# A hybrid encoder block: order of two products in the last token quad of a block pair, weight slots in that order, and a buffer of its own for the row diagonals

## The chip, the cores and the metric

The kernel runs on one core of one Trainium2 chip. The metric is device time in microseconds (us) of one execution; the median of several executions is compared. The engines of the core are TensorE (PE in the profile, with its weight loads as PEld), VectorE (DVE), ScalarE (ACT), GpSimd (POOL) and the queues that issue DMAs (SPq on SyncE, ACTq on ScalarE).

## What is computed

One layer over 2048 tokens of width 1024. All groups read one normalised input through one combined projection, each is multiplied by its gate, and an output projection, a residual and a last norm follow. Cut to what matters here:

```python
h = rmsnorm(x, norm_g[l])
proj = h @ w_in[l]
qk_raw, v, o, z_a, gates, u, z_b, qc, z_c = jnp.split(proj, _OFFS, axis=-1)
y_a = mlstm_branch(qk_raw, v, o, ig, fg, ...) * jax.nn.silu(z_a)
y_b = pool_branch(u, pool_w[l], pool_scale[l]) * jax.nn.silu(z_b)
y_c = mem_attn_branch(qc, mem, mem_norm_g[l], w_mem_kv[l]) * jax.nn.silu(z_c)   # softmax over 256 memory rows
x = x + jnp.concatenate([y_a, y_b, y_c], axis=-1) @ w_out[l]
return rmsnorm(x, final_norm_g)
```

The columns `v`, `o` and `z_a`, of 512 each, are made token by token (rows of tokens on the partitions); the change is in how their products are ordered.

## The kernel before, in words

**Tiling.** The 2048 tokens are four blocks of 512. Two blocks make a pair, and the projection of a pair is made by a scheme of Strassen's kind: seven products in place of eight for each "quad" (two blocks of tokens by two column blocks, over two halves of the width). The seven products are named by their input form (`A11`, `A12`, `S1`, `S2`, `S3`, `S4`, `A22`) and their weight form (`B11`, `B21`, `T1`, `T2`, `T3`, `B22`, `N4`). `T1` is a plain difference of two weight blocks, `T2` takes `T1` off a third. `S1`, with `T1`, is the input form that is a plain sum. Every fp32 operand is split into a high and a low part, and a product is three matmuls for each tile (`mm3`, lines 151 to 156): high by high, high by low, low by high. A product of a token quad is 48 matmuls: two banks (`bk`), in each two tiles of 128 tokens, four slices of the width and the three parts.

**A token quad** is `run_tok`, lines 390 to 448. It goes through the seven products in the order of a table (`TOK_ORDER`, line 49). A product writes two PSUM banks. `A11` and `A12` accumulate in the banks `P` and `S1` and `S4` in `V`, both under the PSUM tag `mm`, of which there are four banks. `S2` writes `U`, and `S3` and `A22` write `W`, both under the tag `pt`, of which there are two banks. ACT copies `P` away after `A11` into `s1` (line 418) and makes the first output `c11` from it after `A12` (line 421); DVE makes `u2` from `U` after `S2` (line 425) and turns `s1` into `V + u2` after `S1` (line 427); the other three outputs follow at lines 430, 436 and 442, each stored from ACT's queue (line 397). The tags `s1` and `u2` have two buffers each in SBUF; `c11` and the row diagonals `dg` take buffers of `u2` in turn.

**Order.** Per pair: a mixed stage (channel quads with convolution and pooling), then `attention_stage` (line 911) with four attention quads and one token quad, that with index `i == 2` (`z_a`, function Silu). This token quad runs while the softmax of the last head is still under way: `attend` (line 746) puts its scores, its transposes into two `pt` banks (`transposes`, line 770) and its product with the memory values (`pv`, line 785) a counted number of steps ahead (`later`, `tick`). The transposed probabilities are split by ACT (line 781) and DVE (line 782) and leave the `pt` banks by that. The order in which each engine gets its instructions is then made from this program by a planner that runs the program on a simulated clock and takes, on each engine, the earliest written instruction that it holds to be ready (`schedule_with_timeline_sim=True`); a few instructions are tied behind the one written before them on their engine (`keep_in_program_order`).

**Between the pairs.** After the first pair's quad with index 2 comes the first pair's quad with index 1, called with `turn` (line 941): it loads the second pair's raw input (`y`, line 181), multiplies it by the row norms (`scale_y`, line 183) and splits it into the new forms, each into the slots that the old form has just left. The row norms are spread over the partitions by `bcast` (line 163): DVE writes four diagonal blocks into `dg`, and one PE matmul against ones (line 168) puts them into a bank of tag `aux`. `scale_y` runs it twice, for block 2 and for block 3. Then come the second pair's quads 1 and 0. The weight forms of quad 1 are read back from DRAM (line 285) into eight slots (`wf`), of which a form takes two, as slots become free.

**Beside the second pair's quad with index 2** the output weights are loaded and split (`prep_wo`, line 966), into input slots in the order of the table `wslots` (line 963) as the forms `A12`, `S2`, `S1` and so on are done with them.

Of the kernel before, what the change touches and what calls it, by code (L numbers as in the profile page):

```python
# [15 lines left out]
ALU = mybir.AluOpType  # L16
AX = mybir.AxisListType

P = 128
# [28 lines left out]
            ("S1", "T1", "V", True), ("S3", "T3", "W", True), ("S4", "B22", "V", False), ("A22", "N4", "W", False))  # L48
TOK_ORDER = (("A11", "B11", "P", True), ("A12", "B21", "P", False), ("S2", "T2", "U", True),
             ("S1", "T1", "V", True), ("S3", "T3", "W", True), ("S4", "B22", "V", False), ("A22", "N4", "W", False))  # L50


def hybrid_block(tc, xT, xn, memT, wch, wuT, wtok, wgt, wkm, wvm, wo, pw, cols, bg, gf, out):
# [33 lines left out]
    with ExitStack() as outer:  # L87
# [72 lines left out]
            V.tensor_scalar(ms[:, :w], src, 1.0 / n, EPS, ALU.mult, ALU.add)  # L160
            G.tensor_tensor(dst, ms[:, :w], mhalf[:, :w], ALU.pow)

        def bcast(src_cols, w):
            dg = ev("dg", shape=(P, 4, P), tag="u2")
            for i in range(w):
                V.tensor_scalar(dg[:, i], ident, src_cols[:, i:i + 1], None, ALU.mult)
            pb = bank([P, 4, P], "aux")
            tc.keep_in_program_order(T.matmul(pb[:, :w], ones, dg[:, :w], start=True, stop=True))
            return pb[:, :w].rearrange("p a b -> p (a b)")
# [13 lines left out]
        def scale_y(s, y, i, halves=(0, 1)):  # L183
            b = 2 * s + i
            if 0 in halves:
                rbs[b] = bcast(rt[:, 4 * b:4 * b + 4], 4)
            rb = rbs[b]
            for h in halves:
                for k in range(4):
                    g = col[:, C_NG + 4 * h + k:C_NG + 4 * h + k + 1]  # L190
                    V.scalar_tensor_tensor(y[i][h][k], y[i][h][k], g, rb, ALU.mult, ALU.mult)
# [32 lines left out]
        class Quad:  # L224
            def __init__(self, kind, s, i):
                self.kind, self.s, self.i = kind, s, i
                self.tok = kind == "tok"
                self.order = TOK_ORDER if self.tok else CH_ORDER
                self.cost = 2 if self.tok else 1
                self.forms = {}  # L230
                self.held = {}
                self.raw = {}
                self.kept = not (self.tok and i == 0)
# [46 lines left out]
            def prep(self, f):  # L280
# [6 lines left out]
                    self.views(f, out)  # L287
                    return
                B = self.raw
                if f == "T2":  # L290
                    G.tensor_tensor(B["B11"], B["B12"], B["B11"], ALU.subtract)  # L291
                    B["T1"] = B["B11"]
                    t2 = wb.tile([P, 4, 256 if self.tok else P], F32, name="wt2", tag="wt2", bufs=1)
                    V.tensor_tensor(t2, B["B22"], B["T1"], ALU.subtract)
                    B["T2"] = t2
# [94 lines left out]
        def run_tok(q, step=None, pinned=False):  # L390
# [9 lines left out]
            for n, (xfm, wfm, acc, opens) in enumerate(q.order):  # L400
# [5 lines left out]
                for bk in range(2):  # L406
                    pp = banks[acc][bk]
                    for r in range(2):
                        sl = slice((2 * bk + r) * P, (2 * bk + r + 1) * P)
                        for k in range(4):  # L410
                            wh, wl = q.forms[wfm][k]
                            xt = xf[xfm][k]
                            mm3(pp[:, r], xt[:, 0, sl], xt[:, 1, sl], wh, wl, opens and k == 0 and r == 0, k == 3,
                                pin=k == 0 and (opens and r == 1 or pinned and r == 0))
                    pf = pp.rearrange("p a b -> p (a b)")
                    if n == 0:
                        s1[bk] = ev("s1")
                        A.activation(s1[bk], pf, AF.Copy)
                    elif n == 1:
                        c11 = ev("c11", tag="u2")  # L420
                        A.activation(c11, pf, func)
                        store(c11, 0, 0, bk)
                    elif n == 2:
                        u2[bk] = ev("u2")
                        V.tensor_tensor(u2[bk], pf, s1[bk], ALU.add)
                    elif n == 3:
                        V.tensor_tensor(s1[bk], pf, u2[bk], ALU.add)
                    elif n == 4:
                        t = s1[bk]
                        V.tensor_tensor(t, pf, t, ALU.add)  # L430
                        if n_:
                            A.activation(t, t, func)
                        store(t, 1, 1, bk)
                    elif n == 5:
                        t = ev("c12", tag="s1")
                        V.tensor_tensor(t, pf, u2[bk], ALU.add)
                        if n_:
                            A.activation(t, t, func)
                        store(t, 0, 1, bk)
                    else:  # L440
                        t = u2[bk]
                        V.tensor_tensor(t, pf, t, ALU.add)
                        if n_:
                            A.activation(t, t, func)
                        store(t, 1, 0, bk)
                    if bk == 1:
                        used(q, wfm)
                    tick()
# [511 lines left out]
        close(mcm)  # L960

        korder = [8, 7, 9, 6, 10, 5, 11, 4, 0, 1, 2, 3]
        wslots = [8, 10, 4, 6, 12, 14, 16, 18, 20, 22, 24, 26]
        woh, wol = {}, {}

        def prep_wo(i):
# [298 lines left out]
```

## Time and profile before

| | us |
|---|---|
| median of 3 runs | 1219.67 (1218.44 to 1222.29) |
| the profiled execution | 1220.8 |
| its span, first to last instruction | 1218.9 |
| PE busy in it | 1173.5 |
| DVE busy in it | 743.9 |
| ACT busy in it | 480.5 |
| POOL busy in it | 211.5 |
| mean granted TensorE clock | 0.983 |

In the rows below, a timeline row gives the start in us, the duration in us, the engine with the source line, the operation, the tiles (out<-in), how many instructions are merged in the row (x), and in brackets how long the engine had been idle before it and what ended that. Times count from the start of the span. A granted clock of 1.00 is 2.4 GHz.

### The profile page before, as it was taken

What the parts mean: (1) busy time and instruction counts of PE and PEld (TensorE: products, weight loads), DVE (VectorE), ACT (ScalarE), POOL (GpSimd) and SP (SyncE); (2) the same over time, 40 slices, a digit from 0 to 9 for tenths busy, and PEclk for the clock granted to TensorE, in tenths of its full rate; (3) what the DMA queues carried; (4) which work ended last, traced back from release to release, by engine and by line L of the source; (5) the groups of instructions that cost most, each with busy time, mean ns of one, the idle gap of its engine ahead of it and who ended that gap; (6) DMA issues with size and microseconds to landing.
All of it is one profiled execution on the core that took longest, in us unless ns stands there. A gap on an engine that the chain in (4) does not pass through costs nothing. (4 is left out here: it accounts for less than half of the span.)

```text
span 1218.9 us, 17628 instructions
## 1 busy us (share of the span) xinstructions
PE 1173.5 (96%) x6579; PEld 1016.1 (83%) x6579; DVE 743.9 (61%) x1324; ACT 480.5 (39%) x947; POOL 211.5 (17%) x154
## 2 busy tenths in 40 slices
PE   6769999999999999999999999999999999999997
PEld 5759888887888998998788888888978888888886
DVE  5966587887777559633564554554546656556444
ACT  7534544444766444331311225555433223222211
POOL 1351121112001003100000000000054423233110
PEclk9879999999999999999999999999999999999999
DMA  9618788779555796546667776446695454554411
GB/s 350 233 44 299 265 293 281 259 276 324 211 195 182 256 390 226 181 140 228 198 219 241 240 244 226 154 155 223 214 325 188 137 184 154 172 165 151 144 52 69
DMA packets 124725, 258.75 MB, mean 212 GB/s; under 512 B 9824, under 2 KB 66400, under 8 KB 124384
## 3 DMA queue, kind: packets, MB, share of 16 engines
q1 hardware_dynamic: 83232, 226.17, 53.9%
q10 hardware_dynamic: 41408, 31.46, 8.1%
q8 instruction: 52, 0.85, 0.3%
q14 instruction: 33, 0.27, 0.1%
HBM read 158.96 MB, written 98.63 MB: 211 GB/s over the span
## 5 line engine op out<-in xcount | busy, mean ns | idle before, releaser
L307 ACT ACTIVATE wf<-wr 128x512 fp32r<-128x512 f32 x120 | 74.3, 627 | 106.7 <-PE mm L156 56.1
L308 DVE TENSOR_TENSOR wf<-wr,wf 128x512 fp32r<-128x512 f32 x120 | 84.8, 716 | 35.2 <-ACT wf L307 35.1
L152 PE MATMUL mm<-xS,wf 128*128 128x512 f32 x256 | 101.3, 396 | 1.9 <-DVE s L377 1.9
L156 PE MATMUL mm<-xS,wf 128*128 128x512 f32 x256 | 101.7, 397 | 0.0
L155 PE MATMUL mm<-xS,wf 128*128 128x512 f32 x256 | 101.0, 395 | 0.0
L1025 PE MATMUL mm<-woh,ybh 128*128 128x512 f32 x256 | 94.8, 405 | 0.0
L1025 PE MATMUL mm<-wol,ybh 128*128 128x512 f32 x256 | 92.8, 397 | 0.0
L1025 PE MATMUL mm<-woh,ybl 128*128 128x512 f32 x256 | 89.9, 394 | 0.0
L152 PE MATMUL mm<-xA,wf 128*128 128x512 f32 x224 | 88.6, 396 | 0.0
L156 PE MATMUL mm<-xA,wf 128*128 128x512 f32 x224 | 87.9, 393 | 0.0
L155 PE MATMUL mm<-xA,wf 128*128 128x512 f32 x224 | 87.7, 392 | 0.0
L1129 DVE SCALAR_TENSOR_TENSOR hh<-hh,ss,gz 128x128 f32<-128x128 f32 x64 | 52.4, 878 | 31.1 <-POOL ss L1127 31.1
L647 DVE SCALAR_TENSOR_TENSOR cacc<-text,col,cacc 128x1024 f32<-128x1024 f32 x48 | 65.5, 1374 | 6.7 <-ACT cacc L644 6.5
L996 POOL TENSOR_TENSOR ybl<-yr,ybh 128x1024 fp32r<-128x1024 f32 x16 | 39.2, 2450 | 173.2 <-ACT ybh L995 169.7
L291 POOL TENSOR_TENSOR wr<-wr 128x512 f32<-128x512 f32 (+1 forms) x16 | 27.2, 1697 | 198.8 <-DVE wf L308 180.4
L152 PE MATMUL pt<-wf,xS 128*128 128x256 f32 x192 | 55.7, 290 | 5.7 <-ACT xS L198 4.6
L156 PE MATMUL pt<-wf,xS 128*128 128x256 f32 x192 | 55.5, 289 | 5.2 <-DVE xS L199 5.2
L156 PE MATMUL mm<-wf,xA 128*128 128x256 f32 x192 | 56.3, 293 | 3.7 <-DVE xA L199 3.7
L152 PE MATMUL mm<-wf,xA 128*128 128x256 f32 x192 | 57.1, 297 | 2.0 <-DMA wf<-d_tok1B 2.0
L152 PEld LDWEIGHTS mm<-xS,wf 128*128 128x128 f32 x256 | 48.5, 189 | 12.0 <-DVE s L377 2.4
L156 PEld LDWEIGHTS mm<-xS,wf 128*128 128x128 f32 x256 | 48.6, 190 | 10.9
L155 PEld LDWEIGHTS mm<-xS,wf 128*128 128x128 f32 x256 | 48.5, 189 | 10.1
(314 smaller groups left out, 3251.3 us busy)
## 6 DMA issues: line engine op xcount, KB each, us to landing
wr<-in_wch_dram SPq DMA_DIRECT2D x20, 512.0 KB, 5.8
y<-in_xT_dram SPq DMA_DIRECT2D x32, 256.0 KB, 6.9
wr<-in_wtok_dram SPq DMA_DIRECT2D x16, 512.0 KB, 6.0
d_qk<-cacc ACTq DMA_DIRECT2D x32, 256.0 KB, 4.5
yr<-d_y SPq DMA_DIRECT2D x16, 512.0 KB, 4.7
qk<-d_qk SPq DMA_DIRECT2D x16, 512.0 KB, 4.1
gz<-d_t SPq DMA_DIRECT2D x16, 512.0 KB, 3.7
xr<-in_xn_dram SPq DMA_DIRECT2D x16, 512.0 KB, 3.6
```

What stands on the lines that cost most here:

```text
L152: ins = T.matmul(po, ah, bh, start=first, stop=False, skip_group_check=True)
L155: T.matmul(po, ah, bl, start=False, stop=False, skip_group_check=True)
L156: T.matmul(po, al, bh, start=False, stop=last, skip_group_check=True)
L291: G.tensor_tensor(B["B11"], B["B12"], B["B11"], ALU.subtract)
L307: A.activation(t[:, 0], part, AF.Copy)
L308: V.tensor_tensor(t[:, 1], part, r32(t[:, 0]), ALU.subtract)
L647: V.scalar_tensor_tensor(c, t[:, i:i + 2 * BW], w(i), c, ALU.mult, ALU.add)
L996: G.tensor_tensor(yl, yr, r32(yh), ALU.subtract)
L1025: T.matmul(outs[c][n], l, w[:, n * 512:(n + 1) * 512], start=i == 0 and p_ == 0, stop=i == KO - 1 and p_ == 2)
L1129: V.scalar_tensor_tensor(hh[:, h], hh[:, h], ss[:, h:h + 1], gz[:, 1, h], ALU.mult, ALU.mult)
```

## The change

In the token quads with index 2 (one in each pair) `S1` with `T1` is the third product and `S2` with `T2` the fourth; in the other token quads the order stays. The difference `T1` of the weights is made when the first of the two forms is prepared. `s1` becomes `V + u2` after whichever of the two products comes fourth, so in these quads both DVE sums stand behind `S2`. The table of slots for the output weights takes the slots of `S1` before those of `S2`. For the second pair's blocks `bcast` writes its diagonals into a buffer of their own, one for both blocks, in place of a buffer of `u2`.

```diff
--- before.py
+++ after.py
@@ -48,6 +48,7 @@
             ("S1", "T1", "V", True), ("S3", "T3", "W", True), ("S4", "B22", "V", False), ("A22", "N4", "W", False))
 TOK_ORDER = (("A11", "B11", "P", True), ("A12", "B21", "P", False), ("S2", "T2", "U", True),
              ("S1", "T1", "V", True), ("S3", "T3", "W", True), ("S4", "B22", "V", False), ("A22", "N4", "W", False))
+TAIL_ORDER = TOK_ORDER[:2] + (TOK_ORDER[3], TOK_ORDER[2]) + TOK_ORDER[4:]
 
 
 def hybrid_block(tc, xT, xn, memT, wch, wuT, wtok, wgt, wkm, wvm, wo, pw, cols, bg, gf, out):
@@ -160,8 +161,8 @@
             V.tensor_scalar(ms[:, :w], src, 1.0 / n, EPS, ALU.mult, ALU.add)
             G.tensor_tensor(dst, ms[:, :w], mhalf[:, :w], ALU.pow)
 
-        def bcast(src_cols, w):
-            dg = ev("dg", shape=(P, 4, P), tag="u2")
+        def bcast(src_cols, w, own=False):
+            dg = misc([P, 4, P], "dg") if own else ev("dg", shape=(P, 4, P), tag="u2")
             for i in range(w):
                 V.tensor_scalar(dg[:, i], ident, src_cols[:, i:i + 1], None, ALU.mult)
             pb = bank([P, 4, P], "aux")
@@ -183,7 +184,7 @@
         def scale_y(s, y, i, halves=(0, 1)):
             b = 2 * s + i
             if 0 in halves:
-                rbs[b] = bcast(rt[:, 4 * b:4 * b + 4], 4)
+                rbs[b] = bcast(rt[:, 4 * b:4 * b + 4], 4, s > 0)
             rb = rbs[b]
             for h in halves:
                 for k in range(4):
@@ -225,7 +226,7 @@
             def __init__(self, kind, s, i):
                 self.kind, self.s, self.i = kind, s, i
                 self.tok = kind == "tok"
-                self.order = TOK_ORDER if self.tok else CH_ORDER
+                self.order = CH_ORDER if not self.tok else TAIL_ORDER if i == 2 else TOK_ORDER
                 self.cost = 2 if self.tok else 1
                 self.forms = {}
                 self.held = {}
@@ -287,9 +288,10 @@
                     self.views(f, out)
                     return
                 B = self.raw
-                if f == "T2":
+                if f in ("T1", "T2") and "T1" not in B:
                     G.tensor_tensor(B["B11"], B["B12"], B["B11"], ALU.subtract)
                     B["T1"] = B["B11"]
+                if f == "T2":
                     t2 = wb.tile([P, 4, 256 if self.tok else P], F32, name="wt2", tag="wt2", bufs=1)
                     V.tensor_tensor(t2, B["B22"], B["T1"], ALU.subtract)
                     B["T2"] = t2
@@ -413,25 +415,26 @@
                             mm3(pp[:, r], xt[:, 0, sl], xt[:, 1, sl], wh, wl, opens and k == 0 and r == 0, k == 3,
                                 pin=k == 0 and (opens and r == 1 or pinned and r == 0))
                     pf = pp.rearrange("p a b -> p (a b)")
-                    if n == 0:
+                    if xfm == "A11":
                         s1[bk] = ev("s1")
                         A.activation(s1[bk], pf, AF.Copy)
-                    elif n == 1:
+                    elif xfm == "A12":
                         c11 = ev("c11", tag="u2")
                         A.activation(c11, pf, func)
                         store(c11, 0, 0, bk)
-                    elif n == 2:
-                        u2[bk] = ev("u2")
-                        V.tensor_tensor(u2[bk], pf, s1[bk], ALU.add)
-                    elif n == 3:
-                        V.tensor_tensor(s1[bk], pf, u2[bk], ALU.add)
-                    elif n == 4:
+                    elif xfm in ("S2", "S1"):
+                        if xfm == "S2":
+                            u2[bk] = ev("u2")
+                            V.tensor_tensor(u2[bk], pf, s1[bk], ALU.add)
+                        if n == 3:
+                            V.tensor_tensor(s1[bk], banks["V"][bk].rearrange("p a b -> p (a b)"), u2[bk], ALU.add)
+                    elif xfm == "S3":
                         t = s1[bk]
                         V.tensor_tensor(t, pf, t, ALU.add)
                         if n_:
                             A.activation(t, t, func)
                         store(t, 1, 1, bk)
-                    elif n == 5:
+                    elif xfm == "S4":
                         t = ev("c12", tag="s1")
                         V.tensor_tensor(t, pf, u2[bk], ALU.add)
                         if n_:
@@ -960,7 +963,7 @@
         close(mcm)
 
         korder = [8, 7, 9, 6, 10, 5, 11, 4, 0, 1, 2, 3]
-        wslots = [8, 10, 4, 6, 12, 14, 16, 18, 20, 22, 24, 26]
+        wslots = [8, 10, 12, 14, 4, 6, 16, 18, 20, 22, 24, 26]
         woh, wol = {}, {}
 
         def prep_wo(i):
```

## Rows read from the trace of the kernel before

**Rows 1.** The page, busy time: us, share of span, instructions.
```profile
PE 1173.5 (96%) x6579; PEld 1016.1 (83%) x6579; DVE 743.9 (61%) x1324; ACT 480.5 (39%) x947; POOL 211.5 (17%) x154
```

**Rows 2.** Waits of PE, whole span: us in total, times, longest.
```profile
PE aux L152 <- ACT th L781: 2.9, 2, 2.0
...
PE mm L152 <- DMA wf<-d_tok1B: 2.0, 1, 2.0
...
PE pt L152 <- DVE u L442: 0.6, 1, 0.6
```

**Rows 3.** Windows, one token product each: busy by engine, granted clock, DMA share, GB/s.
```profile
436.14:441.95 5.81, 5.81 (x52) 5.81 (x51) 2.90 (x5) 2.92 (x5) 0.00 (x0) 1.00 1.05 405
...
464.48:471.81 7.33, 7.33 (x50) 7.33 (x51) 7.33 (x13) 1.74 (x3) 4.30 (x4) 0.77 0.63 241
844.30:851.45 7.15, 7.15 (x50) 7.15 (x51) 2.51 (x3) 2.03 (x2) 0.00 (x0) 0.79 0.95 363
...
406.92:412.65 5.73, 5.73 (x50) 5.73 (x51) 1.23 (x2) 0.60 (x1) 0.00 (x0) 1.00 0.78 276
```

**Rows 4.** Timeline, second pair: after the last softmax's transposes.
```profile
842.92 1.09 ACT L781 ACTIVATE th<-pt 128x512 fp32r<-128x512 f32 x2 [0.48 <-ACT c L421]
...
843.57 0.49 PE L152 MATMUL aux<-th,vmhl 128*128 128x512 f32 x1 [1.99 <-ACT th L781]
...
844.30 0.58 PE L152 MATMUL pt<-wf,xS 128*128 128x256 f32 x1 [0.23 <-DVE tl L782]
```

**Rows 5.** Timeline, first pair: the same place.
```profile
406.15 0.49 PE L152 MATMUL aux<-th,vmhl 128*128 128x512 f32 x1 [0.89 <-ACT th L781]
...
406.92 0.39 PE L152 MATMUL pt<-wf,xS 128*128 128x256 f32 x1 [0.27 <-DVE tl L782]
```

**Rows 6.** Timeline between the pairs: DVE's diagonals, scalings and first sum; PE.
```profile
446.48 0.88 DVE L166 TENSOR_SCALAR dg<-ident,rt 128x128 f32<-128x128 f32 x4 [1.71 <-DMA d_t<-u]
...
450.27 1.02 PE L168 MATMUL aux<-dg,ones 128*128 128x512 f32 x2
...
451.92 5.35 DVE L191 SCALAR_TENSOR_TENSOR y<-y,col,aux 128x512 f32<-128x512 f32 x8
457.19 0.87 DVE L166 TENSOR_SCALAR dg<-ident,rt 128x128 f32<-128x128 f32 x4
...
459.61 1.02 PE L168 MATMUL aux<-dg,ones 128*128 128x512 f32 x2
...
464.48 0.39 PE L152 MATMUL mm<-wf,xA 128*128 128x256 f32 x1 [2.01 <-DMA wf<-d_tok1B]
...
469.26 0.69 DVE L425 TENSOR_TENSOR u<-pt,s 128x512 f32<-128x512 f32 x1
```

**Rows 7.** Timeline between the pairs: ACT's first output, second bank.
```profile
460.67 0.60 ACT L421 ACTIVATE c<-mm 128x512 f32<-128x512 f32 x1 [1.72 <-PE aux L168]
```

**Rows 8.** Stores issued by L397: the one at 442.0, then seven of 430.5 to 461.3.
```profile
L397 ACTq DMA_DIRECT2D d_t<-u x1: 366/366/366, 442.0 to 442.0; - x1
...
DMA to landing us min/median/max: 10.6/10.6/10.6
...
DMA to landing us min/median/max: 6.1/7.7/10.6
```

**Rows 9.** The second pair's input loads: durations, first and last issue, landing.
```profile
L181 SPq DMA_DIRECT2D y<-in_xT_dram x16: 328/558/1180, 418.2 to 435.8; - x16
...
DMA to landing us min/median/max: 3.8/6.1/7.1
```

**Rows 10.** Timeline, second pair: an output weight's split, and the second sum of U.
```profile
850.53 1.06 ACT L977 ACTIVATE woh<-woraw 128x1024 fp32r<-128x1024 f32 x1 [5.12 <-DMA woraw<-in_wo_dram]
851.49 0.69 DVE L425 TENSOR_TENSOR u<-pt,s 128x512 f32<-128x512 f32 x1 [2.03 <-PE pt L156]
```

**Rows 11.** Timeline behind that quad: last output weights, and PE's next wait.
```profile
874.55 1.52 SPq L975 DMA_DIRECT2D woraw<-in_wo_dram  x2
...
887.61 0.60 PE L1083 MATMUL aux<-qk 128*128 128x128 f32 x3 [0.72 <-DMA qk<-d_qk]
```

## The prediction, made before the changed kernel was run

> **What bounds the kernel now.** I read first the busy times on the page: PE works in 96% of the span [rows 1]. A change that takes no matmul away can therefore win only what PE stands still, and what PE runs slowly afterwards. So the second view is the list of what PE waited for [rows 2]. Three of its rows name what this change can touch: the split of the transposed probabilities (`th`, 2.9 us in two waits), the return of a weight form from DRAM (2.0 in one) and an evacuation of bank `W` (0.6 in one). The third view, the timeline, puts them into places; the fourth, windows cut on single products, shows what the clock costs behind them.
>
> *The second pair's last softmax* [rows 4]. PE ends the eight transposes at 843.57 - 1.99 = 841.58 and waits 1.99 us for `th`, runs one matmul of `pv`, waits 0.23 for `tl`, and only then can `S2` write: its banks `U` have the tag `pt`, and both `pt` banks still hold the transposes. The `S2` product that follows runs at a mean granted clock of 0.79 (between the 1.2 and 2.4 GHz levels) and takes 7.15 us; one at 1.00, of another token quad, takes 5.81 [rows 3]. PE had been idle before the fall, so the gap costs another 7.15 - 5.81 = 1.34. This place: 1.99 + 0.23 + 1.34 = **3.56 us**.
>
> *The first pair's last softmax* [rows 5]. The same picture, shorter: 0.89 + 0.27 = **1.16 us**; the product behind it took 5.73 at a clock of 1.00 [rows 3], so nothing is lost to the clock.
>
> *Between the pairs* [rows 6, 7]. DVE's first diagonals wait 1.71 us for a store of the quad before, whose buffer they take. Then eight scalings, the second diagonals, splits, and eight more scalings stand in one row on DVE, and `c11` of the second bank waits 1.72 us for the second broadcast, because it takes the diagonals' buffer. The first `u2` sum comes only at 469.26, long after `S2`, which PE had behind it when it ran the first broadcast at 450.27. Until then the `pt` banks are shut, `S3` cannot start, and PE turns to the next quad's `A11`, whose weights land late: 2.01 us idle. That product then takes 7.33 us at a clock of 0.77; against 5.81 that is 1.52 more [rows 3]. Further on, the late DVE row costs the 0.6 behind `W` [rows 2]. This place: 2.01 + 1.52 + 0.6 = **4.13 us**.
>
> **The change part by part.** *Products exchanged in both quads with index 2.* No instruction is added or taken away. After `A12` comes `S1`, whose banks `V` have the tag `mm`; two of the four `mm` banks are `P`, the other two were left by the last attention quad's sums long before. So PE has 5.8 us of work [rows 3] that needs no `pt` bank. The splits that it waited for end at 842.92 + 1.09 for `th` [rows 4], 2.4 us after the transposes; 5.8 us cover that. I take the whole of both places: 1.16 + 3.56 = 4.72.
>
> *What is next in line there.* Before, `S1` stood between `U` and `W` and gave DVE 5.8 us to empty `U`. Now `S3` writes `W`, in the same two `pt` banks, right behind `S2`. Each bank still has the other bank's half product as cover, 5.81 / 2 = 2.9 us, against an evacuation of 0.69 that started at 851.49, as the product ended [rows 10]. So 2.2 us are to spare, and I book nothing. If the cover fails, the same kind of gap returns (a rival below). `V` waits one product longer for its sum; no one else wants an `mm` bank until the output products.
>
> *Weight forms and slots.* `T1` is prepared a place earlier and `T2` a place later, from the same instructions; in the first pair both lie far ahead in the eight slots. The output weights that waited for `S2`'s input slots now wait for those of `S1`, which is again the third product: nothing. The last of them hang on the slots of `A22`, at 874.55, and PE's next wait, 0.72 at 887.61, hangs on those by DMA [rows 11]: both move with PE, so the gain is not given back there.
>
> *Own buffer for the diagonals.* The eight writes and two broadcasts stay (0.88, 0.87 and 1.02 us a group [rows 6]). Taken away are the wait of 1.71 on the store and the 1.72 of `c11` on the broadcast. The last input load is issued at 435.8 and with the longest landing of 7.1 has come by 442.9 [rows 9], so DVE can scale some 8 us earlier than at 451.92. The old quad's `u2` then comes after the store of `c11` and no longer behind two rows of scalings, `S3` follows `S1`, and PE does not need the late weights at 464.48. I take the whole 4.13. Bounds: from 4.13 gained to a loss. `c11` of the second bank must now wait for the store of the old `u2`, which landed at 442.0 + 10.6 = 452.6 [rows 8], and for its own half of `A12`, which comes within the 8.7 us of `S1` and that half behind the broadcast at 450.27, so at about 456; its store takes 6.1 to 7.7 more [rows 8], so with the sums' own time the second `u2` comes at 463 to 465. PE has old work until about 462 (450.27, a broadcast 1.0, `S1` 5.8, half of `A12` 2.9 and half of `S3` 2.9 make 462.9, less the 1.16 from before). A wait of up to 3.5 with 1.5 of clock may thus come back in place of 4.13, a net loss of 0.9; half of `S4` or the next quad's `A11` can fill it. I take the value at the gaining end, as the fill is written in the same quad and ready.
>
> *A rule against the single buffer.* The two blocks' diagonals had two buffers and now share one, so the second writes wait for the first broadcast. The rows show 457.19 for the second writes, 5.9 us after the first broadcast ended (450.27 + 1.02) [rows 6]; the buffer was not what they waited for. The Trainium skill (Trainium Kernel Development and Optimization, Best Practices) asks for double buffers to overlap work. By that rule the second group would stand bare for at most its own 0.87 and 1.02, and the sum would be 1.9 smaller.
>
> *Sum.* 4.72 + 4.13 = 8.85 against the profiled execution of 1220.8 (span 1218.9 and 1.9 around it): 1211.95, that is 1212 within what follows. The median of the runs lies 1.1 below that execution; I leave the 1.1 for small new waits and name 1212.0.
>
> **The rivals.** About 0.3%, 3.7 us, is what a measurement of this kernel can tell from no change.
> 1. *The middle shuts again.* The wait on `c11`'s stores replaces the wait on the weights, for little or nothing. For it: landings of 7.7 and 10.6 us [rows 8] and a DMA share of 1.05 in the product from 436.14 [rows 3]. Against it: PE has half products to put there. Time: 1220.8 - 4.72 = 1216.1, or 1217.0 with the loss of 0.9.
> 2. *The gap at the second softmax moves behind `S2`.* DVE and ACT split output weights there; ACT waited 5.12 us for one of their loads at 850.53 [rows 10]. If DVE's order puts such a split ahead of the second `u2` sum, `S3` waits for a DMA. The 3.56 are given back: 1220.8 - 8.85 + 3.56 = 1215.5.
> 3. *The change does not do what it says*: the planner still runs `S2` or `pv` first, or moves the wait. 1220.8.
> 4. *Slower: the second broadcast holds PE.* The broadcasts are tied behind the old quad's last matmul and each other, and with the store no longer in the way the planner may place both early on PE. On DVE the second diagonals stood behind eight scalings, 5.35 us [rows 6], and those wait for loads that land until 442.9. PE would then stand for 5.35 + 0.87 = 6.2 us, with 1.5 of clock 7.7, and the 4.13 would not come: 1220.8 - 4.72 + 7.7 = 1223.8. It decides once PE reaches the second broadcast more than about 3.2 us before its diagonals are written. Against it: before, PE came to that broadcast at 459.61 and did not wait [rows 6]. The Trainium skill (Perfetto Trace Analysis, Tensor Engine Instruction) says that DVE, ACT and GpSimd take their instructions strictly in order, so no later write overtakes a scaling that waits; by that rule the 6.2 stands in full, and 469.26, behind the scalings, agrees.
>
> **How the numbers follow.** Forecast 1212.0: 0.45. Rival 1: 0.22. Rival 2: 0.13. Rival 3: 0.08. Rival 4: 0.12. Faster by over 0.3% means below 1217.1: all of the forecast, and about 0.25 of the 0.35 of rivals 1 and 2, whose spread crosses the line: 0.70. Within 0.3%: their other 0.10, rival 3, and a weak form of rival 4: 0.20. Slower: 0.10. The range goes from 1209.5 (the forecast, 1.1 for the median and 1.4 for the waits behind [rows 11], of which 0.72 is shown) to 1218.5 (rival 1 with its loss and 1.5 of clock elsewhere); it leaves out rivals 3 and 4, 0.20.
>
> **What would show it.** The waits of PE on `th` and `tl` in both last softmaxes should be gone, with `mm<-wf,xS` behind the transposes, at a clock of 1.00. Between the pairs, diagonals should be written without a wait on a store, the first `u2` sum should come about 10 us earlier than 469, and the wait on the weights with its 0.77 stretch should be gone. `S3` should start without a wait on line 425. Wrong would be: a wait of PE on `L425` or `L166`, or a clock below 1.00 in new places.

## The result and the profile after

The changed kernel was slower: 1229.22 us (median of 4 runs, 1227.23 to 1229.66) against 1219.91 for the kernel before beside it, a ratio of 1.0066 with a 95% interval of 1.0045 to 1.0087. Timed once more later, it stood at 1226.13 (8 runs) against 1221.48: 1.0037, 1.0021 to 1.0054. The forecast was 1212.0 and the range ended at 1218.5. The profiled execution took 1229.66, with a span of 1227.8. Two runs at a far lower clock, 1678.41 of the version with the tie (0.655) and 1597.56 of the kernel before beside it (0.687), are left out of all medians and ratios below.

The page still shows PE busy in 96% of the span. Columns as in [rows 1]:

```profile
PE 1177.6 (96%) x6579; PEld 1021.1 (83%) x6579; DVE 746.9 (61%) x1324; ACT 482.1 (39%) x949; POOL 212.9 (17%) x154
```

The matmuls are as many as before. Of the 8.9 by which the span grew, 4.1 are busy time of PE and 4.8 are new idle time. The list of what PE waited for in the whole span, columns as in [rows 2]:

```profile
PE aux L1137 <- DVE hh L1132: 6.3, 2, 4.5
...
PE pt L153 <- DVE u L428: 3.8, 1, 3.8
...
PE aux L1086 <- DMA qk<-d_qk: 1.5, 1, 1.5
...
PE mm L1028 <- ACT yah L1140: 0.7, 1, 0.7
```

The waits on `th`, on the weights and on `u` of L442 that stood in [rows 2] are gone. In their place stand a wait on the first sum of `u2` (L428 is L425 of before), and three in the output stage, of which only the one on `qk` was there before, at 0.72 [rows 11]. No wait on `hh` was in the list of the kernel before.

To put the loss into places, I match three evacuations that every version of the kernel has: the last `s1` before the first pair's last softmax, a channel quad's `s1` soon after the pairs are through, and the one before the second pair's last softmax. First the kernel before, then the changed one (start, duration, engine, line, tile):

```profile
398.83 0.59 ACT L418 ACTIVATE s<-mm 128x512 f32<-128x512 f32 x1
590.81 0.60 ACT L367 ACTIVATE s<-mm 128x512 f32<-128x512 f32 x1 [2.27 <-PE mm L156]
834.47 0.59 ACT L418 ACTIVATE s<-mm 128x512 f32<-128x512 f32 x1
```

```profile
399.40 0.60 ACT L420 ACTIVATE s<-mm 128x512 f32<-128x512 f32 x1
595.25 0.60 ACT L369 ACTIVATE s<-mm 128x512 f32<-128x512 f32 x1 [1.99 <-PE mm L157]
838.99 0.60 ACT L420 ACTIVATE s<-mm 128x512 f32<-128x512 f32 x1
```

The changed kernel is later by 0.57, 4.44 and 4.52 at the three, and by 8.9 at the end of the span. So 0.57 is the **start**, which no part of the change touches; 4.44 - 0.57 = 3.87 is lost in the **middle** (the first pair's last softmax, the stretch between the pairs, the gates); nothing in the channel products; and 8.9 - 4.52 = 4.38 in the **tail** (the second pair's last softmax and the output stage). The forecast had -1.16 - 4.13 in the middle and -3.56 in the tail. These three differences are given for each run below, against the traced execution of the kernel before (spans are read to 0.1, so a tail is good to 0.1).

*The second pair's last softmax* came out as forecast. PE's timeline there:

```profile
845.06 0.60 PE L779 MATMUL pt<-ident,pe 128*128 128x128 f32 x4
845.41 0.36 PE L153 MATMUL mm<-wf,xS 128*128 128x256 f32 x1
...
853.13 0.28 PE L153 MATMUL pt<-wf,xS 128*128 128x256 f32 x1
```

`S1` (tag `mm`) stands right behind the first four transposes, `S2` (tag `pt`) after it, and no row carries a wait, where [rows 4] had 1.99 and 0.23.

*Between the pairs* the diagonals are written early and the first `u2` sum still comes late. DVE and PE:

```profile
446.48 1.06 PE L169 MATMUL aux<-dg,ones 128*128 128x512 f32 x2
450.48 5.36 DVE L192 SCALAR_TENSOR_TENSOR y<-y,col,aux 128x512 f32<-128x512 f32 x8
...
464.51 0.68 DVE L428 TENSOR_TENSOR u<-pt,s 128x512 f32<-128x512 f32 x1
465.33 0.36 PE L153 MATMUL pt<-wf,xS 128*128 128x256 f32 x1 [3.82 <-DVE u L428]
```

Both broadcasts now run without a wait of PE (the second at 446.48, 13 us earlier than in [rows 6]), and the sum comes at 464.51 in place of 469.26. PE is there earlier still. The windows of the changed kernel, columns PE, PEld, DVE, ACT, POOL, clock, DMA share, GB/s:

```profile
440.00:470.00 30.00, 26.18 (x197) 25.04 (x196) 30.00 (x44) 15.88 (x28) 9.21 (x6) 0.94 0.77 283
575.00:580.00 5.00, 5.00 (x16) 3.95 (x16) 2.74 (x12) 1.80 (x3) 0.00 (x0) 0.67 0.28 89
905.00:910.00 5.00, 1.05 (x10) 0.86 (x8) 4.90 (x14) 1.61 (x8) 3.75 (x3) 0.94 0.99 345
910.00:915.00 5.00, 3.81 (x12) 2.96 (x13) 4.38 (x12) 0.60 (x1) 2.45 (x3) 0.50 0.51 183
```

and the kernel before in the first of these stretches:

```profile
440.00:470.00 30.00, 27.99 (x207) 26.34 (x206) 23.27 (x43) 13.18 (x23) 2.49 (x2) 0.94 0.90 329
```

DVE is busy in 30.00 of 30 us, against 23.27 before: the own buffer took away a wait of DVE's [rows 6], and DVE filled the time with the next block's work, in an order in which the old quad's sum stands behind eight scalings and a row of splits. On the chip it is this order that holds the sum, not a store: the store of the first bank's `c11`, whose buffer this sum takes in turn, was issued at 452.29 and landed 3.1 us later, 9 us before the sum.

*The output stage* took the most. The first chunk's numerators (L1101), VectorE's small scaling (L1129), GpSimd's power (L1130) and split (L999), and the transposes of `hh` (L1137), in the changed kernel:

```profile
899.35 1.05 PE L1101 MATMUL pt<-vt,Dm 128*128 128x129 f32 x8
903.14 1.04 ACT L998 ACTIVATE ybh<-yr 128x1024 fp32r<-128x1024 f32 x1
904.31 2.35 POOL L999 TENSOR_TENSOR ybl<-yr,ybh 128x1024 fp32r<-128x1024 f32 x1 [6.27 <-ACT ybh L998]
904.51 2.18 DVE L1129 TENSOR_SCALAR ss<-ss 128x4 f32<-128x4 f32 x1
906.77 1.02 POOL L1130 TENSOR_TENSOR ss<-ss,mhalf 128x4 f32<-128x4 f32 x1
908.96 2.19 DVE L1132 SCALAR_TENSOR_TENSOR hh<-hh,ss,gz 128x128 f32<-128x128 f32 x4
910.50 0.45 PE L1137 MATMUL aux<-ident,hh 128*128 128x128 f32 x1 [4.45 <-DVE hh L1132]
```

The same in the kernel before (three lines less in the numbering):

```profile
894.79 1.06 PE L1098 MATMUL pt<-vt,Dm 128*128 128x129 f32 x8
899.33 0.17 DVE L1126 TENSOR_SCALAR ss<-ss 128x4 f32<-128x4 f32 x1 [1.00 <-ACT sq L1125]
899.58 1.03 POOL L1127 TENSOR_TENSOR ss<-ss,mhalf 128x4 f32<-128x4 f32 x1 [2.72 <-DVE ss L1126]
900.82 1.13 DVE L1129 SCALAR_TENSOR_TENSOR hh<-hh,ss,gz 128x128 f32<-128x128 f32 x4
903.68 2.36 POOL L996 TENSOR_TENSOR ybl<-yr,ybh 128x1024 fp32r<-128x1024 f32 x1 [3.08 <-PE pt L1098]
904.54 0.60 PE L1134 MATMUL aux<-ident,hh 128*128 128x128 f32 x4
```

Nothing of this was edited, but the orders differ. PE has some 14 output matmuls of the second chunk ahead of the first chunk's numerators that stood behind them before. GpSimd splits the fourth chunk's `y` (2.35) ahead of the small power (1.02) on which `hh` hangs; before, the power came first. VectorE's scaling, 0.17 before, took 2.18 and ended with that split. The scaling of `hh` starts 8.1 us later (4.5 of that is the lag from the stages ahead) and takes 2.19 in place of 1.13; its transposes on PE start 6.0 later. PE waits 4.45, and from 910 to 915 it runs at a granted clock of 0.50, the level of 1.2 GHz.

### The profile page after: what moved, and what is told of

It reads as the page before. It is cut to its first block, busy times and chain, and to the rows that moved or that the text cites. A ratio compares the mean times of both kernels' runs of the same rounds, so it can differ in the third digit from the quotient of the medians.

```text
span 1227.8 us, 17633 instructions
## 1 busy us (share of the span) xinstructions
PE 1177.6 (96%) x6579; PEld 1021.1 (83%) x6579; DVE 746.9 (61%) x1324; ACT 482.1 (39%) x949; POOL 212.9 (17%) x154
## 5 line engine op out<-in xcount | busy, mean ns | idle before, releaser
L999 POOL TENSOR_TENSOR ybl<-yr,ybh 128x1024 fp32r<-128x1024 f32 x16 | 38.9, 2436 | 176.2 <-ACT ybh L998 151.4
L157 PE MATMUL mm<-wf,xA 128*128 128x256 f32 x192 | 55.7, 291 | 3.7 <-DVE xA L200 3.7
L1028 PEld LDWEIGHTS mm<-woh,ybl 128*128 128x128 f32 x256 | 48.0, 188 | 10.7
```

Of the source, the lines that this page charges most:

```text
L157: T.matmul(po, al, bh, start=False, stop=last, skip_group_check=True)
L999: G.tensor_tensor(yl, yr, r32(yh), ALU.subtract)
L1028: T.matmul(outs[c][n], l, w[:, n * 512:(n + 1) * 512], start=i == 0 and p_ == 0, stop=i == KO - 1 and p_ == 2)
```

## The experiments

My theory after the result: the exchange does in the tail what was forecast, and loses more than that to the order that the planner then gives the output stage; in the middle, VectorE takes over from the weights as what PE waits for. The rivals: the own buffer or the exchange itself costs time in place; or the matmuls that filled the softmax are simply missing later, so that no order helps. For each run a line gives the differences at start, middle and tail, worked out as above, and how long PE stood in the middle (the sum of the waits in its timeline from the first landmark to the second; 3.78 before, 4.00 after).

**The parts alone.** Four versions: the own buffer alone; the exchange in the first pair, in the second pair, in both, without the own buffer.

```
-    self.order = CH_ORDER if not self.tok else TAIL_ORDER if i == 2 else TOK_ORDER
+    self.order = CH_ORDER if not self.tok else TAIL_ORDER if i == 2 and s == 0 else TOK_ORDER
```

> Only the diagonals' own buffer; the products keep the old order in all quads. Theory A (the loss lies in two places: in the middle, brought by the own buffer, and in the output stage, brought by the second pair's exchange): the middle alone, about +5.3 us by the trace of the change against before between 435 and 825 us, so some 1225; the waits behind the second softmax stay at 1.99 and 0.23, the output stage keeps its one wait of 0.72 on qk and 1.23 on Cn. Theory B (the exchange is to blame for everything, the own buffer is harmless or wins): 1216 to 1220.

> Only the exchange in the first pair's quad with index 2; diagonals in the old buffers, second pair and slots as before. Theory A: PE's waits of 0.89 and 0.27 behind the first softmax go, about -1.3, and the rest is as before: 1218.5. Theory B: the exchange also upsets the order between the pairs, 1222 to 1225.

> Only the exchange in the second pair's quad, with its slot order. Theory A: 1.99 + 0.23 + the slow product go (-3.6 to -4.0), and the output stage loses 8.4 through waits of PE on hh: +4.4, 1224. Rival C (the output stage's loss comes from the phase in which PE arrives there, so from the middle, and not from the exchange): -3.6, 1216.

> Both exchanges and the slot order, diagonals in the old buffers. Theory A: -1.3 -4.0 +8.4 = +3.1, about 1223, with the hh waits in the output stage and the old 2.01 on the weights in the middle. Theory B: as slow as the whole change, 1229. Rival C: 1215.

| kernel | us | ratio to before (95%) | start | middle (PE stood) | tail |
|---|---|---|---|---|---|
| own buffer alone | 1223.76 | 1.0031 (1.0015 to 1.0047) | +0.5 | +4.4 (9.05) | -1.4 |
| exchange, first pair | 1224.82 | 1.0027 (1.0003 to 1.0052) | +2.9 | +3.6 (7.30) | -2.4 |
| exchange, second pair | 1224.37 | 1.0033 (1.0016 to 1.0051) | -1.0 | +0.2 (4.37) | +3.9 |
| exchange, both pairs | 1230.24 | 1.0076 (1.0051 to 1.01) | -1.3 | +4.1 (6.16) | +4.0 |

Each part costs about 0.3% by itself. The tail turns to +4 in the versions with the exchange in the second pair and in no other, also where the middle is as before (+0.2), so rival C falls. The own buffer and the first pair's exchange lose in the middle, each by itself; in the changed kernel, which has both, the losses do not add up (the traces further down). By the times, theory A holds for the own buffer and for the second pair's exchange, theory B for the first pair's exchange and for both. In the run with the first pair's exchange, PE's 1.16 come back longer at the weights, and the second softmax (not exchanged there) waits as before:

```profile
468.88 0.58 PE L153 MATMUL mm<-wf,xA 128*128 128x256 f32 x1 [5.43 <-DMA wf<-d_tok1B]
...
849.77 0.50 PE L153 MATMUL aux<-th,vmhl 128*128 128x512 f32 x1 [1.67 <-ACT th L784]
850.50 0.39 PE L153 MATMUL pt<-wf,xS 128*128 128x256 f32 x1 [0.22 <-DVE tl L785]
```

The wait on the weights was 2.01 [rows 6], now 5.43. With the own buffer alone it goes, but PE waits 1.50 on the first `u2` sum, 2.71 on the sum that makes the last output (L445), and 2.44 here, on a split by ACT:

```profile
470.88 0.35 PE L153 MATMUL mm<-wf,xS 128*128 128x256 f32 x1 [2.44 <-ACT xS L199]
```

A second thing follows from these traces. The 1.67 + 0.22 at 849.77 are nearly the gap of [rows 4], but the product behind it ran at full clock (window of PE: length, busy, clock, DMA share, GB/s):

```profile
849.77:855.00 5.23, 5.00 (x40) 1.00 1.06 401
```

The fall to 0.79 that I had booked as part of the gap came in one of four traces with such a gap (2.22 in the kernel before, 1.85 to 1.97 in the other three). It is the larger part of why the tail is 1.4 to 2.4 shorter even where nothing in it was changed; the rest goes with waits of PE that are 0.5 to 0.8 shorter in sum, those at the softmax and on `qk`.

**The order of the output stage.** The changed kernel with one line's effect: the second chunk's output matmuls from the fifth on are issued behind the first chunk's last numerator matmul. It orders instructions of TensorE alone. GpSimd's power then stands ahead of the split by itself, and VectorE and ScalarE have the order of the kernel before through the whole output stage.

```
+    if c == 0 and i >= 4:
+        with tc.issue_after(pn0[3]):
+            out_k(c + 1, i, ybs[c + 1])
```

> The changed kernel, with one tie in the output stage and nothing else: the second chunk's output matmuls from the fifth on are issued behind the first chunk's last numerator matmul, as the order of the kernel before has them by itself. Theory A (the 8.4 us that the output stage lost come from the order that the planner put there once the second pair's products were exchanged): the waits on hh, 4.45 and 1.83, on yah, 0.69, and the stretch at a clock of 0.69 go, and the time falls from 1229.2 by 6 to 8 to 1221 to 1223. Theory B (the matmuls that PE took forward to fill the last softmax are simply missing later, whatever the order): the waits return elsewhere in the output stage and the time stays at 1227 or above.

Measured: 1216.77, ratio to before 0.9972 (0.9946 to 0.9998), so 12.4 less than the changed kernel, more than either theory had. Start -1.4, middle -0.1 (2.67), tail **-3.55**. The waits on `hh` and `yah` are gone. GpSimd's rows:

```profile
894.12 1.03 POOL L1130 TENSOR_TENSOR ss<-ss,mhalf 128x4 f32<-128x4 f32 x1 [1.11 <-DVE ss L1129]
899.12 2.36 POOL L999 TENSOR_TENSOR ybl<-yr,ybh 128x1024 fp32r<-128x1024 f32 x1 [3.97 <-PE pt L1101]
```

Against the tail of +4.38 this is 7.9 us from an order alone: 5.6 of it are waits of PE (8.47 in this tail before the tie, 2.88 with it), the rest goes with the stretch at 0.50, which is gone. Theory A holds; B falls. The other 4.5 of the 12.4 cannot come from the tie; the two traces differ by more than that in front of it, at the start and in the middle, and the second trace of the changed kernel below shows what that is.

The second version puts only GpSimd's split behind the power and leaves PE's numerators late:

```
+    if c == 3:
+        with tc.issue_after(pw0[0]):
+            G.tensor_tensor(yl, yr, r32(yh), ALU.subtract)
```

> The changed kernel with another tie alone: GpSimd's split of the fourth chunk's y is issued behind the first chunk's small power, which it overtakes in the changed kernel; TensorE's order up to the first hh transposes stays as in the changed kernel. If GpSimd's queue is what makes hh late (the split took 2.35 us ahead of the power, and a VectorE operation of 0.17 took 2.18 beside it), the 4.45 falls to below 1 and the time to 1223 to 1225. If TensorE's late numerators are what makes it late, the wait falls by the 2.4 us of the split at most and stays above 2: 1226 to 1228.

Measured: 1220.48, 0.9993 (0.9972 to 1.0014); start -0.2, middle +0.1 (4.44), tail +0.17. The power, the split, VectorE's scaling of `hh`, and PE:

```profile
900.45 1.03 POOL L1134 TENSOR_TENSOR ss<-ss,mhalf 128x4 f32<-128x4 f32 x1 [5.83 <-PE pt L1104]
901.45 2.34 POOL L1001 TENSOR_TENSOR ybl<-yr,ybh 128x1024 fp32r<-128x1024 f32 x1
...
901.51 3.21 DVE L1136 SCALAR_TENSOR_TENSOR hh<-hh,ss,gz 128x128 f32<-128x128 f32 x4
...
904.09 1.17 PE L1141 MATMUL aux<-ident,hh 128*128 128x128 f32 x4 [2.33 <-DVE hh L1136]
```

The wait is as the second half of the expectation had it, the time below both. This tie is worth 4.38 - 0.17 = 4.2. The other 3.7 are not a clean price of PE's late numerators: the split now runs beside the scaling of `hh`, which takes 3.21 in place of 1.13, so up to 2.1 of the remaining wait of 2.33 go with the split's new place. How the 7.9 divides between GpSimd's order and PE's is therefore not shown; that an order brings them is.

**The middle.** The second bank's `c11` goes to a spare buffer in the quad between the pairs, so that the sums' two buffers turn freely; once alone, once with the tie.

```
-    c11 = ev("c11", tag="u2")
+    c11 = ev("c11", tag="e" if bk and step and not pinned else "u2")
```

> The changed kernel; only in the quad between the pairs the second bank's c11 goes to a spare buffer in place of one of the two that the u2 sums share. Theory A (the new wait of 3.82 us on the u2 sum comes from these two buffers, whose stores hold VectorE's order): the wait goes, the slow stretch behind it too, and the place gives 3.8 to 5.3: 1224 to 1225.5. Theory B (VectorE is simply full there with the scalings and splits of the next block): the first u2 sum is late anyway and the time stays within 1.5 of 1229.2. Where a new wait on the weight forms comes up instead, as in the run with the exchange alone, it gives 1 to 2.

> The changed kernel with both: the tie of the output matmuls and the second bank's c11 in the spare buffer. If the two losses are what was named and independent, the two gains add up: 7 and 4.5 off 1229.2 make 1217 to 1219, below the kernel before by 0.1 to 0.2%. If they feed on one another (time won in the middle is given back at the weight forms or in the output stage), 1221 to 1224.

Measured: alone 1228.02, 1.0052 (1.003 to 1.0074), start +5.4, middle -0.4 (3.14), tail +4.7. With the tie 1219.15, 0.9983 (0.996 to 1.0005), start -0.8, middle -0.4 (2.68), tail -3.54. The first sum of `u2` moves forward. With the tie alone, then with the spare buffer and the tie:

```profile
461.40 0.68 DVE L428 TENSOR_TENSOR u<-pt,s 128x512 f32<-128x512 f32 x1
```

```profile
453.59 0.68 DVE L428 TENSOR_TENSOR u<-pt,s 128x512 f32<-128x512 f32 x1
```

It now stands right behind the eight scalings, no longer behind another 8.8 us of splits and sums, and PE's wait on it goes, as theory A has it. The shared buffers thus go into the place that the planner gives the sum in VectorE's order, though on the chip the store had landed long before (455.4 against 464.51 in the changed kernel). The time does not come (1219.15 against 1216.77 with the tie alone; alone, 1228.02 is within theory B's 1.5 of 1229.2): PE now waits one product later, again on VectorE. From the run without the tie (with it the same 1.45, at 477.96):

```profile
483.81 0.38 PE L153 MATMUL pt<-wf,xA 128*128 128x256 f32 x1 [1.45 <-DVE s L433]
```

The tails, +4.7 and -3.54, repeat what the tie is worth: 8.2.

> The changed kernel with the tie of the output matmuls; it leaves out the eight scalings of the second block of the second pair (5.36 us of VectorE between 450.5 and 455.8), so its time is not that of the whole computation. Theory A (VectorE's full order holds the u2 sum that TensorE waits for between the pairs): the wait of 2.67 to 4.26 on the u2 sum goes, with the slow stretch behind it, and the middle gives 3 to 5: 1213 to 1215. Theory B (the store of c11 holds it): the sum stays where it is, at about 464.5 less the start, and the time at 1217 to 1218.

Measured without the eight scalings, with the tie: 1219.66, 0.9982 (0.9959 to 1.0004); start -0.7, middle +0.4 (3.35), tail -3.1. The first `u2` sum came at 459.22 in place of 461.40, so VectorE's work ahead of it is part of what held it; the wait of 2.67 to 4.26 and the slow stretch went. But four smaller waits took over, the longest of them on the second sum:

```profile
470.79 0.38 PE L153 MATMUL pt<-wf,xS 128*128 128x256 f32 x1 [1.33 <-DVE u L430]
```

So theory A names the right engine and the wrong price: even with 5.4 us of VectorE's work left out, PE stood 3.35 there. (This trace also has the slower pace told of at the end, 2.3 us of its middle.) The three traces in which this stretch was loosened end between 2.68 and 3.35; what sets that floor I did not find.

**The changed kernel again.** It has the same instructions in the same order as the tied version on every engine up to the output stage, so the 3.9 us between their middles asked for a second trace.

> The changed kernel once more, unaltered, for a second trace and more times. The run with the tie has the same instructions in the same order up to the output stage, yet its trace is 3.9 us shorter between the first softmax and the second pair's first channel product (idle 2.67 against 4.00, token products 150.65 against 153.16). Theory A (that is spread between executions of one program): the second trace may lie anywhere between, the waits of 4 to 4.5 on hh and the slow stretch behind them come again, and the median lies at 1225 to 1229. Theory B (the changed kernel has it always): the same stage takes 195 to 196 again and the median is 1229.

Measured: 1226.13, 1.0037 (1.0021 to 1.0054). Start +4.3, middle -0.55 (3.77), tail +4.45. The tail repeats to 0.1, with its wait:

```profile
909.09 0.30 PE L1137 MATMUL aux<-ident,hh 128*128 128x128 f32 x1 [3.70 <-DVE hh L1132]
```

The middle does not: +3.87, -0.09, +0.05 and -0.55 in four traces of one order. Theory A holds. The first trace's loss there belongs to that execution, and the start varies from -1.4 to +5.4 over all runs. The exchange in the second pair alone and its version with the tie, further down, also have one order up to the output stage, with +0.2 and +3.0 in the middle. A middle read from one trace can thus be off by 3 to 4 us.

**The gates.** In the changed kernel's first trace the clock fell to 0.67 at 575 (window above), behind a row of 17 gate matmuls. The kernel before, with all 32 gate matmuls of the second pair tied behind the last token product:

```
+    with tc.issue_after(lt):      # lt: the last token product's last matmul
+        fn()                      # one of the four gate products
```

> The kernel before, with one tie: the second pair's 32 gate matmuls are all issued behind the last token product; 22 of them stood between products in the middle. Where traces had 17 or more of them in a row there (four of five such), the granted clock fell to 0.67 to 0.85 in the ten us that follow and the channel products took 24.3 to 24.4 in place of 23.0; with 10 to 15 in a row it never did. Theory A (the long run of gate matmuls, or what follows it, brings the clock down): a dip at 570 to 585 in the trace, 1.3 to 1.5 lost. Theory B (chance): no dip. Beside it the middle loses its fill: 22 matmuls of 0.23 that stood in the waits of the u2 sums leave up to 3.3 idle there, so 1220 to 1225 in all.

Measured: 1225.82, 1.0038 (1.0017 to 1.006); start +0.5, middle +8.0 (7.96), tail -2.3. The fall came:

```profile
580.00:585.00 5.00, 5.00 (x22) 0.67 0.15 58
```

Of the 8.0, 7.96 - 3.78 = 4.2 are new idle time: these matmuls were fill for the waits of the middle. The fall cost 1.5 (the channel products up to the second landmark took 24.4 in place of 23.0), and 2.4 more went into the token products, which ran at the slower pace told of at the end. For the clock the evidence is mixed. The expectation counted four of five long rows with a fall, and left out the run with the own buffer alone, 21 in a row and none. Over all traces the fall stands behind 5 of 9 rows of 17 or more, and behind none of 5 rows of 10 to 15. A long row does not force a fall; that it takes part in one is not shown.

**The exchange in the second pair alone, with the tie.** The version with the part of the change that paid.

> The exchange in the second pair alone, with the tie of the output matmuls and nothing else of the change: no own buffer, the first pair as before. Theory A (the exchange brings what was forecast for it, 3.56, and lost it to the order of the output stage alone): the waits on th and tl and on hh are all gone and the time is 1220.1 less 3 to 4, 1216 to 1217.5. Theory B (the output stage keeps part of the loss: the wait on qk grew from 0.72 to 1.45): 1218 to 1219.5.

Measured: 1218.97 against 1221.48, 0.998 (0.9965 to 0.9996), so 2.5 less than the kernel before. Start +0.4, middle +3.0 (4.25), tail -3.34. The second pair's waits on `th` and `tl` and the one on `hh` are gone, the one on `qk` is 1.23. The 1218.97 is in theory B's range, but the kernel before stood 1.4 above the 1220.1 of the expectation here, and with that taken off it lies between the theories: the tail has nearly the 3.56, but against other executions of the kernel before, whose tail has no fall of the clock, 1 to 2 of that is no gain. This version and the tied one are faster than both kernels, than the one before by 0.2 and 0.3%, with intervals that end just below no difference. Its middle of +3.0 has 2.3 of the slower pace.

## Why the prediction was wrong

1. **Products exchanged, the softmax.** Right: the waits of [rows 4, 5] went, `S1` covered the splits, `S3` had its bank in time, and with the order kept the tail gave 3.55 for a forecast of 3.56. That they meet to 0.01 is luck: PE's waits in that tail are 1.49 shorter (2.22 at the softmax less 0.73 on `qk`), the clock term is 1.34, and where the other 0.7 come from I did not find. And the sum was made against one execution, and its clock term of 1.34 was that execution's. Tails in which nothing was changed were 1.4, 2.4 and 2.3 shorter. The results list the mean granted clock of every run: 0.983 in the profiled one of the kernel before, above that in 82 of 85 others, with a median of 0.985. Against those tails the exchange is worth about 1 to 2, not 3.56.

2. **"Both move with PE, so the gain is not given back there."** This is the step that failed, and it decided the sign. I had followed what hangs on the last output weights [rows 11] and found only the wait on `qk`, which grew from 0.72 to 1.50 as it might. I took the orders behind as fixed. They are laid out anew by the planner when something ahead of them moves: the exchange in the second pair alone turned PE's and GpSimd's order some 50 us later, and this cost 7.9 us (tail +4.38 to +4.45 without the tie, -3.55 with it; with that exchange alone +3.9 and -3.34).

3. **Between the pairs, 4.13.** Rival 1 came true in its effect: the middle shut again. The weights' wait went and the wait on `u2` took its place, 2.67 to 4.26 in the four traces of that order, and three of the four have a middle within 0.6 of the kernel before, where 1.16 + 4.13 were forecast. A second step failed here, the choice of the gaining end "as the fill is written in the same quad and ready": PE had used it up by 461.5, close to the 462.9 of that working less the 1.16. The 463 to 465 were worked out for the second bank's sum and rest on a store of 6.1 to 7.7; the first bank's sum came then, at 464.5, by chance, and the second only at 476.3. What I had not seen is why: not the store, which had landed at 455.4, but DVE, busy in all of the 30 us, and its order. The 1.16 of the first pair (1.33 measured as PE's lead at 435) were given back here too: before, PE stood 3.78 from the first softmax on, and after it 2.67 to 4.44. The clock terms, 1.52 here, came back as well (0.94 over 440 to 470 in both).

4. **The rule on the single buffer.** The second diagonals stood bare in neither trace of the changed kernel, so the 1.9 did not come. What the Trainium skill asks for there (Trainium Kernel Development and Optimization, Best Practices) is that DMA overlaps with compute; I had carried it over to two engines. The row's reading was right, and rival 4 did not come: PE came to the second broadcast at 446.48 without a wait.

5. **The other rivals.** Rival 2 did not come: no wait stands behind `S2`. Rival 3 did not come either: PE ran `S1` first. The loss by the order of a later stage was in no case; the 0.10 for slower rested on another mechanism.

What stays open: why the four runs of the first timing lie 3 us above the eight of the second (single traces differ by as much at the start and in the middle); what PE would need between the pairs to stand less than 2.7; and how the 7.9 divides between PE's order and GpSimd's.

## What to carry to other kernels

Where a planner sets the order on each engine, an edit moves more than its own instructions: compare the planned orders of all engines from the edit to the end, and look for a small operation on a long chain that a large one now overtakes. A tie that gives the old order nearly back cost nothing here and was worth 7.9 us. And a clock term read from one execution is a chance, not a price: count it only if several executions show it.

## What was not expected of the hardware

*VectorE beside GpSimd.* VectorE's scaling of 4 elements took 2.18 in place of 0.17, from 904.51 to 906.69, while GpSimd's split ran from 904.31 to 906.66; four scalings took 3.21 in place of 1.13 beside the next such split, from 901.45 to 903.79. The small scaling ended as the split did. In the kernel before, beside the split from 903.68, an operation of VectorE with its input in PSUM took its usual 0.16 (L1117, at 904.30), and one with both inputs in SBUF took 1.05 and ended with the split (L1119, 905.01 to 906.06); in the changed kernel it took 0.15 while GpSimd stood idle (901.09). The Trainium skill (SBUF — State Buffer, SBUF: two separate sides) says that the two engines share a pair of ports, locked for a whole instruction by whichever starts first, for operations of VectorE in a two-port mode or with two inputs in that memory. These rows agree, if the small scaling counts among the former.

*Two paces of one product.* At a granted clock of 1.00, a token product took one of two times in these traces. The kernel before, and the changed one, 48 matmuls in either (all engines' columns as in the windows above):

```profile
508.43:514.04 5.61, 5.61 (x52) 5.61 (x51) 3.58 (x5) 2.05 (x4) 2.40 (x1) 1.00 0.26 102
```

```profile
507.81:513.63 5.82, 5.82 (x52) 5.82 (x51) 3.80 (x6) 2.02 (x4) 2.40 (x1) 1.00 0.10 33
```

From 416 to 440 all 14 traces have the slower pace. From about 505 to 564 ten have 5.61 and four 5.82, without a change in between; of the four traces of one order, three have the one and one the other. Over the eleven products of that stretch it makes 11 x 0.21 = 2.3 us, the larger part of what sets the first trace's middle apart. What sets the pace stays open.
